# Layer norms of finished rows moved from VectorE to ScalarE and GpSimd in the second-last expert list, and their stores to GpSimd's queue

## The chip, the cores and the metric

The kernel runs on one core of a Trainium2 chip. The metric is device time in microseconds, the median of three runs. The core's engines each work through a queue of their own in order and wait for each other by semaphores: TensorE (PE, with its weight loads as PEld), VectorE (DVE), ScalarE (ACT), GpSimd (POOL), and SyncE (SP), which here only begins transfers.

## The reference

Two layers of an encoder, 512 tokens of width 1024 in float32. What matters here is the end of the second layer, a mixture of experts:

```
x = layer_norm(DN_ALPHA * x + mix, ln_attn_g[i], ln_attn_b[i])
ffn = moe_swiglu(x, w_router[j], b_router[j], w_exp_in[j], w_exp_out[j])   # top 2 of 8 experts
x = layer_norm(DN_ALPHA * x + ffn, ln_ffn_g[i], ln_ffn_b[i])

def layer_norm(x, g, b):
    mu  = mean(x);  var = mean((x - mu) ** 2)
    return (x - mu) * rsqrt(var + LN_EPS) * g + b
```

Each token goes to two of the eight experts; an expert is a SwiGLU with weights of 1024 x 5632 and 2816 x 1024 in float32.

## The kernel before

**Lists.** Tokens are gathered by expert into eight lists of at most CAP[s] rows (160, 128, 152, 134, 144, 140, 168, 128), and the kernel works list by list. List 6 (L6 = LAST - 1) has 168 places, in two blocks of 128 and 40 rows, and list 7 (LAST) has 128.

**Weights.** All weights are streamed from HBM in chunks of 1 MB (128 x 2048 float32, tile raw). SP begins a load when a raw buffer is free. ACT rounds a chunk to float16 (wh, L149), DVE makes the remainder (wl, L158: raw x 256 minus wh), each in two pieces of 1048 and 1000 columns, and PE does three float16 products for each float32 one. DVE's wl also frees the raw buffer. In list 6 and 7 a list has 22 chunks for the gate and up product (block4 and quad: lines 1442 to 1444) and 11 or 12 for the down product (down_wide, lines 1471 to 1473; down_direct, lines 1517 to 1519, in list 7).

**Activations of a list.** For four columns blocks at a time ACT takes Silu out of PSUM (sa, L1457), DVE multiplies by the up half (L1458), ACT rounds to float16 (act, L231), and GpSimd makes the remainder (L1460). sa has two buffers, so ACT's L1457 waits for a L1460 of two quads earlier.

**Ends of lists.** A list's rows are scaled and added to a table in HBM, expert_sums, by an indirect DMA from GpSimd (add_rows, L1375). When list 6 begins, expert_sums holds lists 0 to 5. In list 6 GpSimd adds it to all four token tiles (token_sums), DVE takes their statistics (stats), and norm_out(t) norms each tile of 128 tokens and stores it to the output. That is done at four places in list 6's program: with its last gate pair and with its first three groups of the down product. The tokens of list 6 and list 7 get wrong values there and are written again: rows_done(L6, i) norms the rows of list 6 after their own down product and writes them over the output (L1691, indirect), at two places in list 7's down product, and rows_done(LAST, 0) does so for list 7 at the very end.

**The two ways to norm.** `inverse` makes 1/sqrt(var + eps): a Sqrt on ACT and five tiny operations on DVE. Then, in halves of 512 columns:

```
def centred(o, mean, inv, gb, n):          # on DVE: (o - mean) * g, then (o * inv) + b
    for h in range(2):
        centre(o, mean, gb, n, h)          # L442
        stretch(o, inv, gb, n, h)          # L446
def shared(o, mean, inv, gb, n=128):       # off = -mean * inv on DVE (L456), then for each half
    nc.scalar.activation(o[:, c], o[:, c], AF.Identity, bias=off, scale=inv)    # L459, ACT
    nc.gpsimd.tensor_mul(o[:, c], o[:, c], gb[0][:n, c])                        # L460, GpSimd
    nc.gpsimd.tensor_add(o[:, c], o[:, c], gb[1][:n, c])                        # L461, GpSimd
```

`shared` is used before already, for two token tiles of the first layer and through norm_rows(..., spread=True). The order of every engine's work is that of the program: nothing reorders it.

Of the kernel before, what the change touches and what calls it, by code (L numbers as in the profile page):

```python
# [56 lines left out]
LAST = NEXP - 1  # L57
# [152 lines left out]
def trunk_kernel(ctx, tc, x, mem, positions, w_in_swa, attn_sinks, w_in_fox, b_forget, w_mem_kv, w_out,  # L210
                 ln_attn_g, ln_attn_b, w_ffn_in, w_ffn_out, w_router, b_router, w_exp_in, w_exp_out,
                 ln_ffn_g, ln_ffn_b, out):
    nc = tc.nc
# [117 lines left out]
    xtok = base.tile([128, NT, D], FT, name="xtok")  # L331
# [76 lines left out]
    def ln_load(lnp, g, b, eng=nc.scalar, **kw):  # L408
        t = []
        for name, w in (("lng", g), ("lnb", b)):  # L410
            o = lnp.tile([128, D], FT, **(kw or {"name": name}))
            eng.dma_start(o, bass.AP(tensor=w.tensor, offset=w.offset, ap=[[0, 128], [1, D]]))
            t.append(o)
        return t
# [11 lines left out]
    def inverse(w, var, s, between=()):  # L426

        between = list(between)
        nc.scalar.activation(w[:, 1], var, AF.Sqrt, bias=eps[s][:var.shape[0]])
        nc.vector.tensor_scalar(w[:, 0], var, EPS / (s * s), None, op0=OP.add)  # L430
        for f in between[:1]:
            f()
        nc.vector.reciprocal(w[:, 1], w[:, 1])
        for f in between[1:]:
            f()
        nc.vector.tensor_mul(w[:, 2], w[:, 1], w[:, 1])
        nc.vector.scalar_tensor_tensor(w[:, 2], w[:, 2], -0.5, w[:, 0], op0=OP.mult, op1=OP.mult)
        nc.vector.scalar_tensor_tensor(w[:, 3], w[:, 2], 1.5, w[:, 1], op0=OP.add, op1=OP.mult)

    def centre(o, mean, gb, n, h):  # L440
        c = slice(h * 512, h * 512 + 512)
        nc.vector.scalar_tensor_tensor(o[:, c], o[:, c], mean, gb[0][:n, c], op0=OP.subtract, op1=OP.mult)  # L442

    def stretch(o, inv, gb, n, h):
        c = slice(h * 512, h * 512 + 512)
        nc.vector.scalar_tensor_tensor(o[:, c], o[:, c], inv, gb[1][:n, c], op0=OP.mult, op1=OP.add)  # L446

    def centred(o, mean, inv, gb, n):
# [4 lines that stand above are left out]
    def shared(o, mean, inv, gb, n=128):  # L453

        off = small.tile([128, 1], FT, name="off")[:n]
        nc.vector.scalar_tensor_tensor(off, mean, -1.0, inv, op0=OP.mult, op1=OP.mult)  # L456
        for h in range(2):
            c = slice(h * 512, h * 512 + 512)
            nc.scalar.activation(o[:, c], o[:, c], AF.Identity, bias=off, scale=inv)  # L459
            nc.gpsimd.tensor_mul(o[:, c], o[:, c], gb[0][:n, c])  # L460
            nc.gpsimd.tensor_add(o[:, c], o[:, c], gb[1][:n, c])  # L461

    def norm_rows(o, st, s, gb, n, spread=False):
        mv = small.tile([128, 2], FT, name="mv")[:n]
        nc.vector.bn_aggr(mv, st)
        w = small.tile([128, 4, 1], FT, name="lnw")[:n]
        if spread:
            inverse(w, mv[:, 1:2], s)
            shared(o, mv[:, 0:1], w[:, 3], gb, n)
        else:  # L470
            inverse(w, mv[:, 1:2], s, [lambda h=h: centre(o, mv[:, 0:1], gb, n, h) for h in range(2)])
            for h in range(2):
                stretch(o, w[:, 3], gb, n, h)
# [507 lines left out]
    gb = ln_load(fp, ln_ffn_g[0], ln_ffn_b[0])  # L981
# [3 lines left out]
    for r in range(0, S + CMAX, 128):  # L985
        m = min(128, S + CMAX - r)
# [338 lines left out]
    def small_t(name, shape, dt=FT):  # L1325
        return me.tile(shape, dt, name=name)
# [5 lines left out]
    def blocks(s):  # L1332
        return [(r, min(128, CAP[s] - r)) for r in range(0, CAP[s], 128)]
# [307 lines left out]
    gbx = ln_load(mx, ln_ffn_g[1], ln_ffn_b[1])  # L1641
# [15 lines left out]
    X = {}  # L1657
# [29 lines left out]
    def rows_done(s, i, st, to):  # L1687

        m = blocks(s)[i][1]
        norm_rows(X[s][i][:m, :], st[:m, :], 1.0, gbx, m)  # L1690
        nc.gpsimd.indirect_dma_start(out=out[0], out_offset=bass.IndirectOffsetOnAxis(ap=to[:m, i:i + 1], axis=0),  # L1691
                                     in_=X[s][i][:m, :], in_offset=None, bounds_check=S - 1, oob_is_err=False)

# [3 lines left out]
    mvs = small_t("mvs", [128, NT, 2])  # L1697
    lnw = small_t("lnw4", [128, 4, NT])
# [5 lines left out]
        nc.vector.bn_aggr(mvs[:, t, :], st)  # L1704

    def norm_out(t, gb):
        centred(xtok[:, t, :], mvs[:, t, 0:1], lnw[:, 3, t:t + 1], gb, 128)
        nc.scalar.dma_start(out[0, t * 128:(t + 1) * 128, :], xtok[:, t, :])

    jobs = {}  # L1710

# [6 lines left out]
    for t in range(NT):  # L1718
        at(L6, 5, lambda t=t: token_sums(t))
        at(L6, 7 if t < 2 else 8, lambda t=t: stats(t))  # L1720
        at(L6, 10 + t, lambda t=t: norm_out(t, gbx))
    at(L6, 9, lambda: inverse(lnw, mvs[:, :, 1], 1.0))
    at(L6, 9, lambda: residual(LAST, rows))
    for i in range(len(blocks(L6))):
        at(LAST, 11 + i, lambda i=i: rows_done(L6, i, st6[:, i, :], at_[L6][1]))
# [7 lines left out]
    for s in range(NEXP):  # L1733
# [41 lines left out]
        else:  # L1775
            for gi, u in enumerate(u_eo[s]):
# [17 lines left out]
                for f in jobs.get((s, 11 + gi), ()):  # L1794
                    f()
    late_work()
    rows_done(LAST, 0, st7, at_[LAST][1])
    mxx.close()

# [4 lines left out]
    with tc.If(nit > 0, preferred_fallthrough_block=False):  # L1804
# [77 lines left out]
        gbx = ln_load(lp, ln_ffn_g[1], ln_ffn_b[1])  # L1882
# [6 lines left out]
        for t in range(NT):  # L1889
            norm_out(t, gbx)  # L1890
# [26 lines left out]
```

## Time and profile before

| | |
|---|---|
| median of 3 runs | 1634.07 us (1633.24 to 1634.15) |
| the profiled execution: its time, its span | 1634.23 us, 1632.4 us |
| PE busy | 1578.6 us (97%) |
| DVE busy | 1210.9 us (74%) |
| ACT busy | 950.3 us (58%) |
| POOL busy | 267.7 us (16%) |

All times of rows are microseconds from the start of the span. The shares are means over stages with different limits: DVE's 74% is near 100% in the last lists. The chain that the page follows back from the last instruction is cut off after the last store, so the end is read from the stages instead. PE's busy time counts overlapping matmuls; a gap in it is real.

### The profile page before, as it was taken

The numbers are of one execution on the slowest core, as the hardware profiler recorded it, in microseconds if no ns is written. First come the engines' busy times: TensorE is split into PE (matmuls) and PEld (weight loads), VectorE is DVE, ScalarE is ACT, GpSimd is POOL, SyncE is SP. The second block draws the span as 40 slices with busy tenths as digits, with TensorE's granted clock in tenths as the row PEclk, the third lists the DMA queues.
The fourth block names the chain that finished last, engine by engine and source line by source line (L and its number), as shares of the span: only waits on it lengthen the run. The fifth ranks groups of instructions, "written<-read, shape, count | busy, mean of one in ns | idle before, by whom it ended". The sixth has DMA issues, their size and how long they took to land. (4 is left out here: it accounts for less than half of the span.)

```text
span 1632.4 us, 42978 instructions
## 1 busy us (share of the span) xinstructions
PE 1578.6 (97%) x18640; PEld 1267.8 (78%) x18640; DVE 1210.9 (74%) x1811; ACT 950.3 (58%) x1447; POOL 267.7 (16%) x264
## 2 busy tenths in 40 slices
PE   7998999999999999999899999999999999999996
PEld 6775654444444747765899999999999999999984
DVE  6798543333634568787898798888979889699997
ACT  6676243333211356663676787767877678666773
POOL 0443100000200000003120330203112030130251
PEclk9999999999999999999999999999999999999998
DMA  7511043332631132201899899999999999999993
GB/s 275 178 53 53 27 129 104 103 104 91 219 114 60 53 129 92 66 27 65 308 363 364 293 394 377 352 370 305 390 357 361 375 320 373 329 297 360 358 369 113
DMA packets 180549, 370.16 MB, mean 227 GB/s; under 512 B 6589, under 2 KB 49597, under 8 KB 180352
## 3 DMA queue, kind: packets, MB, share of 16 engines
q1 hardware_dynamic: 173280, 343.48, 58.6%
q0 software_dynamic: 4768, 15.47, 4.0%
q10 hardware_dynamic: 2304, 8.39, 1.4%
q8 instruction: 148, 2.42, 0.6%
q14 instruction: 49, 0.40, 0.1%
HBM read 355.08 MB, written 12.39 MB: 225 GB/s over the span
## 5 line engine op out<-in xcount | busy, mean ns | idle before, releaser
L158 DVE SCALAR_TENSOR_TENSOR wl<-raw,wh 128x1048 f16<-128x1048 f32 (+3 forms) x658 | 794.7, 1258 | 100.3 <-ACT wh L149 100.1
L149 ACT ACTIVATE wh<-raw 128x1048 f16<-128x1048 f32 (+3 forms) x658 | 641.8, 1036 | 101.7 <-PE bk L239 42.9
L1444 PE MATMUL bk<-xa,wl 128*128 128x160 f16 (+3 forms) x1280 | 260.0, 231 | 0.9 <-DVE wl L158 0.9
L1442 PE MATMUL bk<-xa,wh 128*128 128x160 f16 (+3 forms) x1280 | 260.1, 231 | 0.8 <-ACT xa L231 0.8
L1443 PE MATMUL bk<-xa,wh 128*128 128x160 f16 (+3 forms) x1280 | 260.0, 231 | 0.0
L1443 PEld LDWEIGHTS <-wh 128*128 128x128 f16 x2560 | 250.5, 98 | 3.6 <-issue 2.4
L1444 PEld LDWEIGHTS <-wl 128*128 128x128 f16 x2560 | 250.5, 98 | 1.3 <-DVE wl L158 1.1
L1442 PEld LDWEIGHTS <-wh 128*128 128x128 f16 x2560 | 250.4, 98 | 0.7
L1473 PE MATMUL bk<-act,wl 128*128 128x160 f16 (+6 forms) x1232 | 235.3, 227 | 1.2 <-DVE wl L158 1.2
L1472 PE MATMUL bk<-act,wh 128*128 128x160 f16 (+6 forms) x1232 | 235.3, 227 | 0.0
L1471 PE MATMUL bk<-act,wh 128*128 128x160 f16 (+6 forms) x1232 | 235.2, 227 | 0.0
L1442 PE MATMUL bk<-xe,wh 128*128 128x128 f16 (+2 forms) x1280 | 223.2, 221 | 2.2 <-DVE sa L1458 1.4
L1443 PE MATMUL bk<-xe,wh 128*128 128x128 f16 (+2 forms) x1280 | 223.1, 221 | 0.0
L1444 PE MATMUL bk<-xe,wl 128*128 128x128 f16 (+2 forms) x1280 | 223.1, 221 | 0.0
L237 PE MATMUL bk<-xTh,wh 128*128 128x512 f16 (+2 forms) x656 | 204.8, 322 | 1.2 <-DVE Kx L234 0.9
L239 PE MATMUL bk<-xTh,wl 128*128 128x512 f16 (+2 forms) x656 | 204.6, 322 | 1.4 <-DVE wl L158 1.4
L238 PE MATMUL bk<-xTl,wh 128*128 128x512 f16 (+2 forms) x656 | 204.6, 322 | 0.5 <-DVE xTl L234 0.5
L1460 POOL TENSOR_TENSOR act<-sa,act 128x512 f16<-128x512 f32 (+6 forms) x40 | 106.3, 2659 | 284.7 <-ACT act L231 284.6
L239 PEld LDWEIGHTS <-wl 128*128 128x128 f16 x944 | 92.4, 98 | 49.0 <-DVE wl L158 2.9
L237 PEld LDWEIGHTS <-wh 128*128 128x128 f16 x944 | 92.4, 98 | 48.7 <-ACT wh L149 2.0
L238 PEld LDWEIGHTS <-wh 128*128 128x128 f16 x944 | 92.5, 98 | 46.6 <-issue 1.5
L1473 PEld LDWEIGHTS <-wl 128*128 128x128 f16 x1232 | 120.5, 98 | 1.6 <-DVE wl L158 1.6
(349 smaller groups left out, 2669.2 us busy)
## 6 DMA issues: line engine op xcount, KB each, us to landing
raw<-in_w_exp_in_dram SPq DMA_DIRECT2D x176, 1024.0 KB
raw<-in_w_exp_out_dram SPq DMA_DIRECT2D x85, 1024.0 KB
raw<-in_w_ffn_in_dram SPq DMA_DIRECT2D x22, 1024.0 KB
raw<-in_w_out_dram SPq DMA_DIRECT2D x8, 1024.0 KB
raw<-in_w_ffn_out_dram SPq DMA_DIRECT2D x8, 1024.0 KB
raw<-in_w_in_fox_dram SPq DMA_DIRECT2D x8, 1024.0 KB
raw<-in_w_in_swa_dram SPq DMA_DIRECT2D x4, 896.0 KB
raw<-in_w_mem_kv_dram SPq DMA_DIRECT2D x3, 1024.0 KB
```

The lines of the kernel that those rows point to most:

```text
L149: self.nc.scalar.activation(h[:, p:e], t[:, p:e], AF.Copy, scale=SW)
L158: self.nc.vector.scalar_tensor_tensor(l, src, SW, h, op0=OP.mult, op1=OP.subtract)
L237: nc.tensor.matmul(o, lh, rh, start=first, stop=False, **kw)
L238: nc.tensor.matmul(o, lh, rl, start=False, stop=False, **kw)
L239: nc.tensor.matmul(o, ll, rh, start=False, stop=last, **kw)
L1442: nc.tensor.matmul(o, wh[:, k, c], xe[0][:, k, :C], start=first, stop=False, skip_group_check=True)
L1443: nc.tensor.matmul(o, wh[:, k, c], xe[1][:, k, :C], start=False, stop=False, skip_group_check=True)
L1444: nc.tensor.matmul(o, wl[:, k, c], xe[0][:, k, :C], start=False, stop=k == KD - 1, skip_group_check=True)
L1460: lambda: nc.gpsimd.tensor_sub(act[1][:, j, :C], sa[:, :, :C], act[0][:, j, :C])]
L1471: nc.tensor.matmul(o, wh[:, k, c], act[0][:, kk, :C], start=first, stop=False, skip_group_check=True)
L1472: nc.tensor.matmul(o, wh[:, k, c], act[1][:, kk, :C], start=False, stop=False, skip_group_check=True)
L1473: nc.tensor.matmul(o, wl[:, k, c], act[0][:, kk, :C], start=False, stop=kk == KF - 1, skip_group_check=True)
```

## The change

Two edits. The norm of the four token tiles uses `shared` in place of `centred`, and the store of each tile is begun by GpSimd in place of ACT. And rows_done uses `shared` (spread) for list 6's rows, but not for list 7's.

```diff
     def rows_done(s, i, st, to):
         m = blocks(s)[i][1]
-        norm_rows(X[s][i][:m, :], st[:m, :], 1.0, gbx, m)
+        norm_rows(X[s][i][:m, :], st[:m, :], 1.0, gbx, m, s < LAST)
         nc.gpsimd.indirect_dma_start(out=out[0], ...
...
     def norm_out(t, gb):
-        centred(xtok[:, t, :], mvs[:, t, 0:1], lnw[:, 3, t:t + 1], gb, 128)
-        nc.scalar.dma_start(out[0, t * 128:(t + 1) * 128, :], xtok[:, t, :])
+        shared(xtok[:, t, :], mvs[:, t, 0:1], lnw[:, 3, t:t + 1], gb)
+        nc.gpsimd.dma_start(out[0, t * 128:(t + 1) * 128, :], xtok[:, t, :])
```

DVE at the first token tile, in list 6's last gate pair (xtok is the token tile, mvs and lnw its mean and inverse, lng and lnb the norm's weights):

```order
 L158 SCALAR_TENSOR_TENSOR wl<-raw,wh 128x1000
 L158 SCALAR_TENSOR_TENSOR wl<-raw,wh 128x1048
-L442 SCALAR_TENSOR_TENSOR xtok<-xtok,mvs,lng 128x512
-L446 SCALAR_TENSOR_TENSOR xtok<-xtok,lnw_8950,lnb 128x512
-L442 SCALAR_TENSOR_TENSOR xtok<-xtok,mvs,lng 128x512
-L446 SCALAR_TENSOR_TENSOR xtok<-xtok,lnw_8950,lnb 128x512
+L456 SCALAR_TENSOR_TENSOR off<-mvs,lnw_8950 128x1
 L158 SCALAR_TENSOR_TENSOR wl<-raw,wh 128x1000
```

One tiny operation stands where four of 128 x 512 stood; the same holds at the other three tiles, each of which has four wl between it and the next.

GpSimd from list 6's last remainders of act to list 6's rows (the four tiles' pieces are alike; the last tile's end is shown):

```order
+L460 TENSOR_TENSOR xtok<-xtok,lng 128x512
+L461 TENSOR_TENSOR xtok<-xtok,lnb 128x512
+L460 TENSOR_TENSOR xtok<-xtok,lng 128x512
+L461 TENSOR_TENSOR xtok<-xtok,lnb 128x512
+L1708 DMA out_dram<-xtok 128x1024
+L1375 DMA expert_sums<-yr,to 680x1024 x2
+L1460 TENSOR_TENSOR act_23021<-sa,act_23020 128x4x128 x2
 L1683 DMA xg_21598<-expert_sums,idx 128x1024
```

Sixteen operations and four stores now stand in GpSimd's queue ahead of list 6's additions to expert_sums, list 7's remainders of act and list 7's fetch of its sums.

DVE at the second block of list 6's rows, in list 7's down product (xg holds the block's 40 rows):

```order
 L465 BN_AGGR mv<-st_8947 40x2
 L430 TENSOR_SCALAR lnw<-mv 40x1
-L442 SCALAR_TENSOR_TENSOR xg_19598<-xg_19598,mv,lng 40x512
 L433 RECIPROCAL lnw<-lnw 40x1
-L442 SCALAR_TENSOR_TENSOR xg_19598<-xg_19598,mv,lng 40x512
 L436 TENSOR_TENSOR lnw<-lnw 40x1
 L437 SCALAR_TENSOR_TENSOR lnw<-lnw 40x1
 L438 SCALAR_TENSOR_TENSOR lnw<-lnw 40x1
-L446 SCALAR_TENSOR_TENSOR xg_19598<-xg_19598,lnw,lnb 40x512 x2
+L456 SCALAR_TENSOR_TENSOR off<-mv,lnw 40x1
 L158 SCALAR_TENSOR_TENSOR wl<-raw,wh 128x1048
```

The big four leave DVE here too, and with them what DVE did while the Sqrt ran on ACT; on ACT two L459 now stand between that Sqrt and the next wh.

## Rows read from the trace of the kernel before

**Rows 1.** Windows: list 6's down product, list 7's gate, list 7's down product.

```profile
core 0: us, PE busy (x) PEld busy (x) DVE busy (x) ACT busy (x) POOL busy (x), PEclk, DMA share, GB/s
1482.30:1522.10 39.80, 38.56 (x530) 38.16 (x528) 36.49 (x40) 21.85 (x24) 0.00 (x0) 1.00 0.94 338
1522.10:1585.30 63.20, 61.05 (x1075) 60.71 (x1073) 60.42 (x59) 51.19 (x63) 32.93 (x8) 1.00 1.05 366
1585.30:1620.70 35.40, 30.96 (x202) 19.89 (x198) 31.69 (x50) 19.51 (x27) 7.37 (x3) 0.95 0.50 186
```

**Rows 2.** Waits, 1482 to 1621: who waited for whom, total us, times, longest.

```profile
PE bk L1518 <- DVE wl L158: 4.4, 3, 3.9
...
ACT sa L1457 <- POOL act L1460: 3.2, 1, 3.2
...
PE bk L1473 <- DVE wl L158: 1.2, 2, 0.9
```

**Rows 3.** Timeline of PE in list 7's down product: longest wait, last matmul.

```profile
1605.66 0.27 PE L1518 MATMUL bk<-wl,act 128*128 128x256 f16 x1 [3.89 <-DVE wl L158]
...
1620.39 0.27 PE L1519 MATMUL bk<-wh,act 128*128 128x256 f16 x1
```

**Rows 4.** Timeline of DVE, list 7's last quads and list 6's finished rows.

```profile
1574.15 9.16 DVE L158 SCALAR_TENSOR_TENSOR wl<-raw,wh 128x1000 f16<-128x1000 f32 x8
1583.23 0.68 DVE L1458 SCALAR_TENSOR_TENSOR sa<-bk,sa 128x512 f32<-128x512 f32 x1
...
1594.38 0.20 DVE L465 BATCH_NORM_AGGREGATE mv<-st 128x2 f32<-128x12 f32 x1
...
1597.97 2.93 DVE L158 SCALAR_TENSOR_TENSOR wl<-raw,wh 128x488 f16<-128x488 f32 x3
1600.82 0.19 DVE L465 BATCH_NORM_AGGREGATE mv<-st 40x2 f32<-40x12 f32 x1
...
1604.38 4.61 DVE L158 SCALAR_TENSOR_TENSOR wl<-raw,wh 128x1048 f16<-128x1048 f32 x4
...
1612.35 4.08 DVE L158 SCALAR_TENSOR_TENSOR wl<-raw,wh 128x1048 f16<-128x1048 f32 x4
```

**Rows 5.** DVE's timeline at the second token tile (start, us, instructions, idle before).

```profile
1495.34 0.75 DVE L442 SCALAR_TENSOR_TENSOR xtok<-xtok,mvs,lng 128x512 f32<-128x512 f32 x1
...
1498.24 1.20 DVE L158 SCALAR_TENSOR_TENSOR wl<-raw,wh 128x1000 f16<-128x1000 f32 x1
1499.92 3.52 DVE L158 SCALAR_TENSOR_TENSOR wl<-raw,wh 128x1048 f16<-128x1048 f32 x3 [0.48 <-ACT wh L149]
```

**Rows 6.** Source L149, 1490 to 1526 (ns min/median/max; first and last start).

```profile
L149 ACT ACTIVATE wh<-raw x23: 1019/1060/1077, 1490.4 to 1525.0; 128x1048 f16<-128x1048 f32 x12, 128x1000 f16<-128x1000 f32 x11
```

**Rows 7.** Timeline of a shared norm in the first layer: ACT, then POOL.

```profile
149.10 0.29 ACT L429 ACTIVATE lnw<-mv,eps 128x1 f32<-128x1 f32 x1 [2.39 <-DVE mv L465]
150.41 1.52 ACT L459 ACTIVATE xtok<-xtok,off,lnw 128x512 f32<-128x512 f32 x2 [1.01 <-DVE off L456]
...
151.30 1.27 POOL L460 TENSOR_TENSOR xtok<-xtok,lng 128x512 f32<-128x512 f32 x1 [4.85 <-ACT xtok L459]
```

**Rows 8.** Timeline of POOL, list 6's last remainder and list 7.

```profile
1480.44 1.55 POOL L1460 TENSOR_TENSOR act<-sa,act 128x672 f16<-128x672 f32 x1 [15.16 <-ACT act L231]
1530.04 2.47 POOL L1375 DMA_INDIRECT expert_sums<-yr,to  x1 [48.05 <-ACT yr L1493]
1541.47 10.41 POOL L1375 DMA_INDIRECT expert_sums<-yr,to  x1 [8.95 <-issue]
...
1574.97 9.36 POOL L1460 TENSOR_TENSOR act<-sa,act 128x512 f16<-128x512 f32 x1 [9.26 <-ACT act L231]
```

**Rows 9.** Sources L158 (at 1480.6 and 1583.8) and L1460 (whole span), columns as before.

```profile
L158 DVE SCALAR_TENSOR_TENSOR wl<-raw,wh x1: 2517/2517/2517, 1480.6 to 1480.6; 128x1048 f16<-128x1048 f32 x1
...
L158 DVE SCALAR_TENSOR_TENSOR wl<-raw,wh x1: 1554/1554/1554, 1583.8 to 1583.8; 128x1000 f16<-128x1000 f32 x1
...
L1460 POOL TENSOR_TENSOR act<-sa,act x40: 1150/1518/9356, 812.9 to 1584.7; 128x512 f16<-128x512 f32 x10, 128x640 f16<-128x640 f32 x5, 128x608 f16<-128x608 f32 x5, 128x536 f16<-128x536 f32 x5
```

## The prediction, on record before the run

> **What bounds the kernel now.** I read the windows of the last three stages first [rows 1]. In list 6's down product PE is busy 38.56 of 39.80 us, in list 7's gate 61.05 of 63.20, in its down product 30.96 of 35.40. DVE stands close beside it: 36.49, 60.42 and 31.69. The DMA share is near 1 in the first two. So no engine has much to spare. PE idles 1.24 + 2.15 + 4.44 = 7.8 us in all, and that is the most that relief for DVE can give back from PE's side (plus a little clock: the granted share falls to 0.95 in the last window).
>
> The waits say what ends PE's idle time: wl, twice in list 6's down product and three times in list 7's, the longest 3.9 us [rows 2]. PE's timeline puts that one at 1605.66 [rows 3]. DVE's own timeline shows what made wl late [rows 4]: list 6's finished rows took DVE from 1594.38 to 1597.97 and from 1600.82 to 1604.38, and the wl for which PE waits stands behind them. From there on PE follows DVE: the last wl ends at 1612.35 + 4.08 = 1616.4, PE's last matmul starts at 1620.39. How much of these 4.0 us must come after the wl the rows don't show; I give PE 1 us in hand there (bounds 0 and 2). What comes behind 1620.7 is list 7's own norm, which the change leaves alone. So the account is DVE's: what it gains or loses between 1482 and 1616 arrives at the end, less that 1 us.
>
> The sum is made against the profiled execution, 1634.23, which stands 0.16 above the median of the runs. A measurement of this kernel can hardly tell less than 0.2%, some 3.3 us, from no change.
>
> **Edit 1, the four token tiles.**
>
> *Removed from DVE.* One tile's norm lies between 1495.34 and 1498.24, 2.9 us [rows 5]. Four of them: -11.6.
>
> *Added to DVE.* Four off of 128 x 1. A tiny operation takes 0.2 [rows 4]: +0.8.
>
> *Added to ACT.* The pair of L459 took 1.52 [rows 7], in place of the store's issue. ACT itself has time (21.85 busy of 39.80 [rows 1]). But the pair waits for DVE's off, and the next wh are queued behind it, and DVE's next wl but one waits for a wh. After off DVE has one wl of 1.20 in hand [rows 5], while ACT needs 1.52 for the pair and 1.06 for a wh [rows 6]: DVE idles 1.52 + 1.06 - 1.20 = 1.4. Today it idles 0.48 at that place [rows 5], because the store on ACT waits for the norm. So +0.9 a tile, +3.6 (bounds 0, if ACT is already a wh ahead, and +5.6, if all of the 1.4 is new).
>
> *Added to GpSimd.* Sixteen operations of 1.27 [rows 7] and four stores. They run where POOL is busy for 0.00 of 39.80 us [rows 1], so their own length costs nothing. Their price is what they do to DVE's wl. At 1480.44 a remainder of 1.55 us ran on GpSimd [rows 8] and the wl beside it took 2.517 in place of about 1.2: 1.3 more, 0.84 of GpSimd's time [rows 9]. For an operation of 1.27 that is 1.07. GpSimd can lose, too: the remainder at 1574.97 lasted 9.36 us [rows 8] over eight wl in a row and came to its end only when DVE turned to L1458 [rows 4]; the wl behind that one took 1.554, only 0.35 more [rows 9]. The median of the 40 remainders is 1.518 against a longest of 9.356 [rows 9], so most get in quickly and I count two of three at 1.07 and one at 0.35: 0.85 for each operation that meets a wl. DVE runs wl nearly without a break here, so I let 12 of 16 meet one: +10.2 (bounds 0 and 16 x 1.07 = +17).
>
> On this the Trainium skill has a rule ("SBUF — State Buffer", section "Who interferes with whom"): a DVE instruction with two SBUF inputs contends with a GpSimd instruction that reads SBUF, the lock is exclusive, and whichever was issued first holds it for its whole length while the other blocks fully. The trace agrees that one blocks the other (2.517 beside 1.55), but not that order of issue alone decides, since the one at 1574.97 was passed over by wl issued after it. By the rule each of the 12 would cost the full 1.07, 12.8 in place of 10.2.
>
> *The stores.* GpSimd's queue is in order, and each tile's store waits for that tile's last L461; the next tile's operations are queued behind it. The bytes are the same and POOL is otherwise empty until L1375 at 1530.04 [rows 8], so I cost them at nothing; without that cover they belong to the third rival.
>
> Sum of edit 1 on DVE: -11.6 + 0.8 + 3.6 + 10.2 = +3.0.
>
> **Edit 2, list 6's own rows.** The two stretches are 3.59 and 3.56 [rows 4]. Not all of it goes: the aggregate (0.20), the Sqrt on ACT (0.29) and the tiny operations up to off (1.01 [rows 7]) stay, about 1.5, with nothing left on DVE to fill them. Freed: 2 x 2.1 = -4.2. Two L459 on ACT again precede the next wh, with the same gap of 1.4 and no idle time at that place now: +2.8 (bounds 0 and 2.8). Eight operations on GpSimd, of which I let 6 meet a wl: 6 x 0.85 = +5.1 (bounds 0 and 8.6). The write to the output (L1691) comes a few microseconds later, and nothing waits for it before list 7's rows are through. Sum: +3.7.
>
> **Total.** DVE +6.7, less 1 in hand: +5.7, 1634.2 + 5.7 = **about 1640**. The sum changes its sign with the number n of the 24 operations that meet a wl. Without them it is -11.6 + 0.8 + 3.6 - 4.2 + 2.8 = -8.6; 8.6 / 0.85 = 10, with PE's 1 us in hand 11. I count 18. Own range: 14 to 22 of 24, or +2.3 to +9.1: 1636.5 to 1643.5.
>
> **Rivals.**
>
> *1. Faster.* The operations fall into DVE's gaps, the new ones behind off above all, or run beside its L1458 and its adds, and fewer than 7 meet a wl. Then DVE saves some 3 to 8 us and PE's waits of 7.8 shrink [rows 1]. PE's longest gap of 3.89 [rows 3] goes, with its slow matmuls (its granted clock of 0.95 says that a part of that window ran at 1.2 in place of 2.4 GHz [rows 1]): 1634 - 7 = about 1627. For it: the removed 11.6 + 4.2 are certain, the added price isn't. Against: DVE is busy 36.49 of 39.80 and 31.69 of 35.40, so there are few gaps.
>
> *2. No change.* 8 to 12 meet, or ACT is a wh ahead at the tiles (the +3.6 falls away) while the locks cost what I say: 1634 ± 3.
>
> *3. GpSimd starves and becomes the bound.* What happened at 1574.97 happens to half of the sixteen, at some 5 us each (between 1.27 and 9.36 [rows 7, 8]), and the others wait for half a wl: 16 x (0.5 x 5 + 0.5 x 1.9) = 55 us. The first tile comes four wl and a norm, 4 x 1.2 + 2.9 = 7.7, before the second one's 1495.3 [rows 5], so at 1488, and GpSimd is done at 1543. L1375 wants POOL at 1530.04 and list 7's remainders are behind it; ACT's L1457, which already waits 3.2 for them [rows 2], and PE behind it would be some 12 later: about 1646. A start of L1375 also took 10.41 in place of 2.47 among wl [rows 8], so the four stores could add to it. Against: the median of 1.518, and that off and the gap behind it open the lock at every tile.
>
> *4. Strict turns.* Each operation gets in behind the wl that runs, none starves, and each of 18 costs 1.07: 19.3 in place of 15.3, total +9.7, about 1644. The row of 9.36 speaks against it. It is what the rule of the Trainium skill above ("SBUF — State Buffer", "Who interferes with whom") would make of the time.
>
> **Numbers.** My forecast 0.42, strict turns 0.08, starving 0.14, no change 0.18, faster 0.18. The point is the likeliest case's, 1640. The range 1630 to 1647 leaves out most of the faster cases (0.13) and the worst of the starving ones (0.07). Slower by over 0.2%: 0.42 + 0.08 + 0.14 = 0.64, with a little of it within 0.2% and as much of the no-change case beyond it.
>
> **What would show it.** In the new trace: wl of about 2.2 to 2.5 us wherever a L460 or L461 runs beside one, some 12 of them in list 6's down product; DVE idle for 1.4 behind each off, released by ACT's wh; PE's waits for wl in list 6's down product above 1.2 in total; no wait of 3.9 at L1518 but several shorter ones; POOL done with the four tiles before 1530. I am wrong if most wl keep 1.2 (rival 1), if L1375 starts late (rival 3), or if PE never waits for the delayed wl, because it is further behind DVE in list 6 than I take it to be: then edit 1 costs nothing and only edit 2's +3.7 is left.

## The result and the profile after

The change makes the kernel slower: median 1643.3 us (1642.65 to 1646.25, 4 runs) against 1633.65 (1633.15 to 1634.15, 4 runs), ratio 1.006 with a 95% interval of 1.0047 to 1.0072. That is +9.7 us, where the prediction said +5.7 and a range of 1630 to 1647.

The windows of the changed kernel, at the same places of the program as [rows 1], with the end as a fourth:

```profile
core 0 of [0], span 1644.5 us
core 0: us, PE busy (x) PEld busy (x) DVE busy (x) ACT busy (x) POOL busy (x), PEclk, DMA share, GB/s
1484.10:1527.20 43.10, 39.07 (x530) 38.05 (x528) 36.07 (x27) 30.66 (x36) 30.51 (x21) 1.00 0.83 296
1527.20:1592.60 65.40, 62.41 (x1076) 62.09 (x1074) 65.26 (x63) 51.90 (x64) 32.01 (x8) 0.97 1.05 369
1592.60:1629.40 36.80, 31.95 (x201) 20.45 (x198) 30.40 (x41) 21.18 (x29) 19.72 (x11) 0.91 0.46 172
1629.40:1644.50 15.10, 0.00 (x0) 0.00 (x0) 4.51 (x12) 0.77 (x2) 1.00 (x1) 0.63 0.08 31
```

All four stages are longer: 43.1 for 39.8, 65.4 for 63.2, 36.8 for 35.4, and the end, of which the prediction said that the change leaves it alone, 15.1 for 11.7. DVE's busy time in the first window hardly fell (36.07 for 36.49) although four norms of 2.9, 11.6 us in all, left it.

DVE's timeline from the second tile to the third (as [rows 5]), and POOL's beside it:

```profile
1498.60 0.15 DVE L456 SCALAR_TENSOR_TENSOR off<-mvs,lnw 128x1 f32<-128x1 f32 x1
1498.67 1.19 DVE L158 SCALAR_TENSOR_TENSOR wl<-raw,wh 128x1000 f16<-128x1000 f32 x1
1501.31 6.58 DVE L158 SCALAR_TENSOR_TENSOR wl<-raw,wh 128x1048 f16<-128x1048 f32 x3 [1.45 <-ACT wh L149]
1507.81 0.15 DVE L456 SCALAR_TENSOR_TENSOR off<-mvs,lnw 128x1 f32<-128x1 f32 x1
```

```profile
1499.69 1.30 POOL L460 TENSOR_TENSOR xtok<-xtok,lng 128x512 f32<-128x512 f32 x1 [2.75 <-ACT xtok L459]
1501.07 1.27 POOL L461 TENSOR_TENSOR xtok<-xtok,lnb 128x512 f32<-128x512 f32 x1
1502.30 2.29 POOL L460 TENSOR_TENSOR xtok<-xtok,lng 128x512 f32<-128x512 f32 x1
1504.67 2.11 POOL L461 TENSOR_TENSOR xtok<-xtok,lnb 128x512 f32<-128x512 f32 x1
1507.08 0.59 POOL L1708 DMA_DIRECT2D out_dram<-xtok  x1 [0.30 <-POOL xtok L461]
```

One wl follows off, then DVE idles 1.45 until ACT has done its two L459 and a wh (forecast: 1.4). GpSimd's first operation falls into that gap. The other three meet the three wl that follow: these take 6.58 in place of 3.52 [rows 5], 1.02 more for each operation, and GpSimd's own grow from 1.27 to 2.1 and 2.3. Both engines lose when they overlap. None of the 16 tile operations took more than 2.3, so none waited for more than one wl. (GpSimd's spans are rough in the profile; DVE's are the firmer ones.)

The rows of list 6 on DVE, in list 7's down product (as [rows 4]), to the last four wl:

```profile
1599.50 0.19 DVE L465 BATCH_NORM_AGGREGATE mv<-st 128x2 f32<-128x12 f32 x1
...
1600.84 0.16 DVE L456 SCALAR_TENSOR_TENSOR off<-mv,lnw 128x1 f32<-128x1 f32 x1
1600.91 0.66 DVE L158 SCALAR_TENSOR_TENSOR wl<-raw,wh 128x488 f16<-128x488 f32 x1
1603.55 4.29 DVE L158 SCALAR_TENSOR_TENSOR wl<-raw,wh 128x1048 f16<-128x1048 f32 x2 [1.97 <-ACT wh L149]
...
1612.12 6.60 DVE L158 SCALAR_TENSOR_TENSOR wl<-raw,wh 128x1000 f16<-128x1000 f32 x3 [1.33 <-ACT wh L149]
...
1622.08 4.08 DVE L158 SCALAR_TENSOR_TENSOR wl<-raw,wh 128x1048 f16<-128x1048 f32 x4
```

From the aggregate to the wl behind off it is 1.4 (forecast: 1.5), the gaps are 1.97 and 1.33, and the five wl behind them take 10.89 (4.29 + 6.60) where five of 1.2 would take 6.0.

PE's waits from 1480 to 1632 (as [rows 2]):

```profile
PE bk L1518 <- DVE wl L158: 4.1, 2, 2.1
PE bk L1473 <- DVE wl L158: 3.8, 3, 1.8
PE bk L1442 <- DVE sa L1458: 3.0, 1, 3.0
```

The wait of 3.89 [rows 3] is gone, two of 2.1 and 2.0 stand in its place, the waits of list 6's down product have grown from 1.2 [rows 2] to 3.8, and PE's wait for DVE's sa, at the start of list 7's gate, from 1.4 to 3.0. ACT's wait of 3.2 for GpSimd's remainder [rows 2] no longer occurs.

Last, the end. Source L1804 is the branch behind list 7's norm; with this input no list overflows and the block behind it is skipped. EVENT_SEMAPHORE is a wait, and INC_SWDGE_SEM sets the semaphores of GpSimd's transfers forward. GpSimd's rows there, in the changed kernel (ns min/median/max, first and last start):

```profile
L1804 POOLq EVENT_SEMAPHORE  x5: 17/43/2525, 1634.8 to 1635.2; - x5
...
L1804 POOLq INC_SWDGE_SEM  x1: 1187/1187/1187, 1637.7 to 1637.7; - x1
```

In the kernel before:

```profile
L1804 POOLq EVENT_SEMAPHORE  x4: 17/43/43, 1626.1 to 1626.4; - x4
...
L1804 POOLq INC_SWDGE_SEM  x1: 1122/1122/1122, 1626.5 to 1626.5; - x1
```

Before, there were four such waits of at most 43 ns, and the INC_SWDGE_SEM followed 0.8 after the start of list 7's write (L1691, 1625.7). Now a fifth wait of 2.5 us stands between; it ends at 1637.7, and that write landed 3.2 us after its start at 1634.4.

**One account of the two traces.** Three marks on DVE and GpSimd cut the stretch: DVE's first tile, its last four wl, the start of list 7's L1691. From the first tile to the last four wl before took 1612.35 - 1485.30 = 127.05; now 1622.08 - 1488.83 = 133.25: +6.2. From there to list 7's L1691: 1634.41 - 1622.08 = 12.3, before 13.35: -1.0. From there to the end of the span: 10.1, before 6.7: +3.4. Together +8.6. The profiled execution is 3.5 later already at the first tile (1488.83 for 1485.30), ahead of every changed instruction: ACT's L1457 stood 1.8 later at 1441.47 (before: 1439.68), and after that ACT waited 6.8 for raw data at 1466.8 (before: 2.3). This 3.5 is not the change's: e2 below, with the same instructions up to there, reaches the first tile at 1485.88. 3.5 + 8.6 = 12.1 is the difference of the spans, 1644.5 - 1632.4. The medians differ by 9.7; single runs spread over some 3 us.

### The profile page after: what moved, and what is told of

Same layout as the page of the kernel before. It is cut to its first block, busy times and chain, and to the rows that moved or that the text cites. A ratio compares the mean times of both kernels' runs of the same rounds, so it can differ in the third digit from the quotient of the medians.

```text
span 1644.5 us, 43009 instructions
## 1 busy us (share of the span) xinstructions
PE 1582.9 (96%) x18640; PEld 1270.4 (77%) x18640; DVE 1211.9 (74%) x1793; ACT 959.5 (58%) x1459; POOL 307.5 (19%) x292
## 5 line engine op out<-in xcount | busy, mean ns | idle before, releaser
L158 DVE SCALAR_TENSOR_TENSOR wl<-raw,wh 128x1048 f16<-128x1048 f32 (+3 forms) x658 | 810.9, 1282 | 107.1 <-ACT wh L149 107.0
L149 ACT ACTIVATE wh<-raw 128x1048 f16<-128x1048 f32 (+3 forms) x658 | 642.1, 1036 | 97.2 <-PE bk L239 42.4
L1473 PE MATMUL bk<-act,wl 128*128 128x160 f16 (+6 forms) x1232 | 235.4, 227 | 4.0 <-DVE wl L158 3.8
L1460 POOL TENSOR_TENSOR act<-sa,act 128x512 f16<-128x512 f32 (+6 forms) x40 | 114.2, 2854 | 290.5 <-ACT act L231 290.3
L1473 PEld LDWEIGHTS <-wl 128*128 128x128 f16 x1232 | 120.5, 98 | 5.1 <-DVE wl L158 5.1
```

What stands on the lines that cost most here:

```text
L149: self.nc.scalar.activation(h[:, p:e], t[:, p:e], AF.Copy, scale=SW)
L158: self.nc.vector.scalar_tensor_tensor(l, src, SW, h, op0=OP.mult, op1=OP.subtract)
L1460: lambda: nc.gpsimd.tensor_sub(act[1][:, j, :C], sa[:, :, :C], act[0][:, j, :C])]
L1473: nc.tensor.matmul(o, wl[:, k, c], act[0][:, kk, :C], start=False, stop=kk == KF - 1, skip_group_check=True)
```

## Experiments

Theory: DVE's wl are held up where GpSimd's multiplications and additions read the same memory, by about 1 us each, and by the gap behind off; PE follows DVE at the end; and the end itself is longer because of the stores. Rivals: ScalarE's extra work is what costs; PE's slack hides the tiles; the longer end is chance. The table gives, for each run, the account above: M from DVE's first tile to its last four wl (in e8 without the block that is moved behind them), N from there to list 7's L1691, T from there to the end of the span, each against before (127.05, 13.35, 6.7), their sum, and the time as a ratio to the kernel before on the same chip (1634.5 and 1634.4 there).

| run | M | N | T | sum | ratio (95%) |
|---|---|---|---|---|---|
| changed kernel | +6.2 | -1.0 | +3.4 | +8.6 | 1.0060 (1.0047 to 1.0072) |
| e1, skipped block's stores | 0.0 | -0.2 | +3.2 | +3.0 | 1.0018 (1.0009 to 1.0027) |
| e2, changed, block on ACT | +6.2 | -1.4 | +0.9 | +5.7 | 1.0033 (1.0022 to 1.0043) |
| e3, tiles only | +1.6 | -1.4 | +0.8 | +1.0 | 1.0012 (1.0003 to 1.0021) |
| e4, rows only | +4.6 | -1.4 | +0.6 | +3.8 | 1.0018 (1.0009 to 1.0027) |
| e5, no GpSimd work | -3.5 | +0.3 | +0.4 | -2.8 | 0.9973 (0.9961 to 0.9985) |
| e6, memset | -3.5 | +0.3 | +0.8 | -2.4 | 0.9974 (0.9963 to 0.9985) |
| e7, lock alone | +10.9 | -0.6 | +0.4 | +10.7 | 1.0069 (1.0055 to 1.0082) |
| e8, rows behind last wl | -3.5 | 0.0 | 0.0 | -3.5 | 0.9982 (0.9973 to 0.9991) |

T varies by up to 0.9 between runs whose ends are alike; only e1 and the changed kernel stand apart from that. The trace of e3 is that of its fastest run (1633.86, against a median of 1636.91).

### e1: the stores in the block that is skipped

```diff
-    def norm_out(t, gb):
+    def norm_out(t, gb, queue=nc.scalar):
...
-        nc.scalar.dma_start(out[0, t * 128:(t + 1) * 128, :], xtok[:, t, :])
+        queue.dma_start(out[0, t * 128:(t + 1) * 128, :], xtok[:, t, :])
...
         for t in range(NT):
-            norm_out(t, gbx)
+            norm_out(t, gbx, nc.gpsimd)
```

> The kernel before, but the four stores in the block behind the branch at the program's end, which this input skips, are begun by GpSimd; everything that runs is as before. Theory (skipped block): GpSimd then has to wait for list 7's last write before it closes the skipped block, and the tail from that write's start to the end grows from 6.7 to about 10.1 us: +2.5 to +3.4, about 1636.5. Rival (the longer tail comes from the stores that run, or is chance): no change, 1633.7, tail 6.7.

1638.5 us, ratio 1.0018: DVE's work is where it was (M 0.0) and the kernel is slower by 2.9 us by the ratio, by 4.0 by the medians (expected: 2.5 to 3.4). The skipped block calls norm_out too. GpSimd's program at the branch, before (-) and in this run (+), with the semaphores that each row waits for (ISA is the INC_SWDGE_SEM, together with the waits ahead of it):

```
 L1804 COMPARE_AND_BRANCH
-L1804 ISA [waits Pool_49,DMASW4_49,DMASW3_49,DMASW6_49,DMASW2_49,DMASW7_49,DMASW1_49,DMASW0_49]
+L1804 ISA [waits Pool_49,DMASW4_49,DMASW5_49,DMASW3_49,DMASW6_49,DMASW2_49,DMASW7_49,DMASW1_49,DMASW0_49]
```

GpSimd's transfers take eight semaphores in turn (DMASW0 to 7). On the way round the block GpSimd sets forward those that the block would have used, and first waits for each of them. Before, the block had seven such transfers, which left out one semaphore, DMASW5, and that was the one of list 7's last write. With four stores more the block uses all eight. The source view of L1804 in this run:

```profile
L1804 POOLq EVENT_SEMAPHORE  x5: 17/43/43, 1625.8 to 1629.2; - x5
...
L1804 POOLq INC_SWDGE_SEM  x1: 1107/1107/1107, 1629.3 to 1629.3; - x1
```

The waits stretch from 1625.8 to 1629.2, and the INC_SWDGE_SEM comes 3.9 after the start of list 7's write (1625.4, landed 3.7 later) in place of 0.8; what follows moves with it.

### e2: the changed kernel with that block's stores left to ScalarE

```diff
-    def norm_out(t, gb):
+    def norm_out(t, gb, queue=nc.gpsimd):
...
-        nc.gpsimd.dma_start(out[0, t * 128:(t + 1) * 128, :], xtok[:, t, :])
+        queue.dma_start(out[0, t * 128:(t + 1) * 128, :], xtok[:, t, :])
...
         for t in range(NT):
-            norm_out(t, gbx)
+            norm_out(t, gbx, nc.scalar)
```

> The changed kernel, with the skipped block's four stores left to ScalarE. Theory (skipped block): the tail falls back from 10.1 to 6.7 us and nothing else moves: 1643.3 - 3 = about 1640. Rival: 1643. Either way 11 to 13 of the 16 tile operations on GpSimd meet a wl and the stretch of DVE from list 6's last gate pair to the end of its down product is about 3.3 us longer than before.

1640.4, ratio 1.0033. The long wait is gone again, M is the changed kernel's to 0.1:

```profile
L1804 POOLq EVENT_SEMAPHORE  x4: 17/43/43, 1631.5 to 1631.7; - x4
...
L1804 POOLq INC_SWDGE_SEM  x1: 1197/1197/1197, 1631.8 to 1631.8; - x1
```

So the long wait belongs to the stores that don't run. With those that run T is +0.9, which is within what T varies by. In list 6's down product 11 wl took over 1.6 us (before: none), as expected.

### e3 and e4: one edit at a time

e3 is e2 with rows_done of before:

```diff
-        norm_rows(X[s][i][:m, :], st[:m, :], 1.0, gbx, m, s < LAST)
+        norm_rows(X[s][i][:m, :], st[:m, :], 1.0, gbx, m)
```

> Edit 1 alone (the tiles by ScalarE and GpSimd, their stores by GpSimd; the skipped block's stores by ScalarE so that the tail stays short); list 6's rows by DVE as before. Theory (wl late by the lock, no slack on PE): DVE +3.3 us over the four tiles, PE later by about as much: 1636 to 1637. Rival (PE's slack of 2 to 4 us in list 7's gate takes it up): within 1 us of 1633.7.

e4 is the kernel before with the other edit alone:

```diff
-        norm_rows(X[s][i][:m, :], st[:m, :], 1.0, gbx, m)
+        norm_rows(X[s][i][:m, :], st[:m, :], 1.0, gbx, m, s < LAST)
```

> Edit 2 alone (list 6's rows by ScalarE and GpSimd), tiles by DVE as before. Theory: two gaps of about 1.5 us behind off and six or seven wl longer by about 1 us: DVE +4 to +4.6, time 1637 to 1638.5. Rival (the two stretches of 3.6 us that go from DVE are what PE waits for, so PE gains): 1630.

e3: 1636.9, 1.0012, so +2.0 by the ratio: between the two expectations and nearer to the first. e4: 1637.7, 1.0018, as the theory said. Their ratios add up to 1.0030, e2 has 1.0033. PE's waits in e3, then in e4:

```profile
PE bk L1473 <- DVE wl L158: 2.5, 2, 1.8
PE bk L1518 <- DVE wl L158: 2.4, 2, 2.1
```

```profile
PE bk L1518 <- DVE wl L158: 5.7, 4, 1.8
...
PE bk L1473 <- DVE wl L158: 1.3, 2, 0.9
```

The tiles make PE wait earlier (2.5 at L1473 for 1.2) and less later (2.4 at L1518 for 4.4 [rows 2]): part of PE's delay in list 6 is swallowed by the wait that comes anyway in list 7. What is left of it is what DVE is late by there, and DVE gets half of the tiles' price back (below).

### e5 and e6: GpSimd's operations left out, or made to read nothing

In e5 the two lines of GpSimd are left out in `shared` for the four tiles and list 6's rows (the output lacks g and b there); in e6 memset of the same columns stands for each (the output there is zero).

```diff
-    def shared(o, mean, inv, gb, n=128):
+    def shared(o, mean, inv, gb, n=128, bare=False):
...
             nc.scalar.activation(o[:, c], o[:, c], AF.Identity, bias=off, scale=inv)
-            nc.gpsimd.tensor_mul(o[:, c], o[:, c], gb[0][:n, c])
-            nc.gpsimd.tensor_add(o[:, c], o[:, c], gb[1][:n, c])
+            if not bare:
+                nc.gpsimd.tensor_mul(o[:, c], o[:, c], gb[0][:n, c])
+                nc.gpsimd.tensor_add(o[:, c], o[:, c], gb[1][:n, c])
+            for _ in range(2 * bare):
+                nc.gpsimd.memset(o[:, c], 0.0)
```

(The last two lines are e6's only. The four tiles and list 6's rows pass bare=True.)

> As e2_block_on_act, but GpSimd's multiplication by g and addition of b are left out for the four tiles and list 6's rows (so the output lacks g and b there); ScalarE's part, the gaps behind off and all stores stay. Theory (the lock is what costs): the wl keep 1.2 us, DVE loses 11.6 + 4.2 us and gains 0.8 + 4 to 5 of gaps at the tiles and 2.8 at the rows, net -8; PE's waits for wl shrink: 1628 to 1631. Rival (what costs is ScalarE, whose two L459 delay the next wh): as e2, 1639 to 1641.

> As e5_no_gpsimd_work, but in place of each left out multiplication and addition GpSimd sets the same 512 columns to zero, an operation that writes and reads nothing (the output of these rows is zero before later rows are written over it). Theory (GpSimd's reads and DVE's second input exclude each other): no wl above 1.3 beside these, time as e5, 1628 to 1631. Rival (any GpSimd operation on the same memory holds DVE up): wl of 2 us and more, time as e2, about 1640.

1630.5 and 1631.0, ratios 0.9973 and 0.9974: both faster than before, by the same, though ScalarE does all that it does in e2 and the gaps of 1.45 behind off are there. The wl of e6 in list 6's down product (source L158 from 1484 to 1528), and the four memsets of a tile on POOL:

```profile
L158 DVE SCALAR_TENSOR_TENSOR wl<-raw,wh x27: 1183/1195/1252, 1483.2 to 1527.3; 128x1000 f16<-128x1000 f32 x14, 128x1048 f16<-128x1048 f32 x13
```

```profile
1494.84 2.15 POOL L464 MEMSET xtok<- 128x512 f32 x4 [5.28 <-ACT xtok L459]
```

No wl is longer than 1.252. So ScalarE is not the cost; GpSimd's multiplications and additions are. That they cost because they read is shown by few events: a memset takes 0.52 where a multiplication takes 1.27, and 14 of the 24 memsets (16 at the tiles, 8 at the rows) lie wholly where DVE runs no wl, most of them in the gap behind off. Five lie beside a wl for nearly their whole length, at 1496.46, 1502.61, 1508.75, 1595.89 and 1602.16, and five more for 0.2 to 0.3. None of these wl took longer than 1.252, where a wait would have added up to 0.5. The time of e6 says no more than that of e5. DVE came out 3.5 earlier at its last wl, not 8 as the theory counted: with the wl at their old length DVE runs out of work (in e6 it idles 4.2 ahead of list 6's first join) and being earlier brings no more.

### e7: the lock alone

```diff
     def norm_out(t, gb):
         centred(xtok[:, t, :], mvs[:, t, 0:1], lnw[:, 3, t:t + 1], gb, 128)
+        for h in range(2):
+            for _ in range(2):
+                nc.gpsimd.tensor_mul(spill, xtok[:, t, h * 512:h * 512 + 512], gb[0][:, h * 512:h * 512 + 512])
         nc.scalar.dma_start(out[0, t * 128:(t + 1) * 128, :], xtok[:, t, :])
...
+    spill = small_t("spill", [128, 512], FH)
```

> The kernel before, and behind each of the four tile norms GpSimd multiplies four times 512 columns of the tile by g into a scratch tile that nobody reads (half-precision result): 16 GpSimd operations without any work taken from DVE or given to ScalarE. Theory (lock): nearly all 16 meet a wl and make it about 1.0 us longer, DVE +13 to +16 in list 6's down product; with some 1.5 us that PE has in hand at the end and up to 2 that DVE gets back in list 7's gate: 1643 to 1647. Rival (GpSimd's work lies beside DVE's): 1634.

1645.5, ratio 1.0069: 16 operations that nobody waits for cost 11 us. POOL at the second tile, the wl from 1484 to 1528, and PE's wait:

```profile
1498.46 7.74 POOL L1710 TENSOR_TENSOR spill<-xtok,lng 128x512 f16<-128x512 f32 x4 [4.22 <-issue]
```

```profile
L158 DVE SCALAR_TENSOR_TENSOR wl<-raw,wh x15: 1234/2259/2317, 1483.6 to 1525.9; 128x1048 f16<-128x1048 f32 x8, 128x1000 f16<-128x1000 f32 x7
```

```profile
PE bk L1473 <- DVE wl L158: 10.5, 4, 3.5
```

The median wl is 2.26 for 1.2, and PE's waits in list 6's down product are 10.5 for 1.2. DVE's stretch from the first tile to list 6's first join is 12.6 longer (expected: 13 to 16), and 1.7 of it comes back in list 7's gate (expected: up to 2).

### e8: list 6's second block behind the last wl

```diff
     L6 = LAST - 1
+    LATE = (0, 3)
...
-        at(LAST, 11 + i, lambda i=i: rows_done(L6, i, st6[:, i, :], at_[L6][1]))
+        at(LAST, 11 + LATE[i], lambda i=i: rows_done(L6, i, st6[:, i, :], at_[L6][1]))
```

> The kernel before, with the norm of list 6's second block of rows moved from the second to the fourth place of list 7's down product, which puts it behind DVE's last wl. Theory (DVE's 3.56 us between two wl is what PE's 3.9 us wait in list 7's down product is made of, and DVE idles 3.3 us behind its last wl): the wait falls below 1.5 and the time to 1631 to 1632.5. Rival (the 3.56 us then delay DVE's last joins by as much): no change or up to 2 slower.

1631.4, ratio 0.9982 (0.9973 to 0.9991): faster than both kernels, as expected. DVE's end and PE's wait:

```profile
1607.99 4.08 DVE L158 SCALAR_TENSOR_TENSOR wl<-raw,wh 128x1048 f16<-128x1048 f32 x4
1611.99 0.19 DVE L465 BATCH_NORM_AGGREGATE mv<-st 40x2 f32<-40x12 f32 x1
...
1615.55 0.47 DVE L1506 SCALAR_TENSOR_TENSOR xg<-bk,g,xg 128x256 f32<-128x256 f32 x1
```

```profile
PE bk L1518 <- DVE wl L158: 0.9, 3, 0.3
```

The 3.56 us of the second block now fill the time in which DVE idled behind its last wl, and PE's longest wait in that stage is 0.3 for 3.9. With the wait the fall of PE's clock is gone: the granted clock of the same stage is 1.00 here, against 0.95 before [rows 1], where it fell to 1.2 GHz right behind the wait of 3.89.

## Why the prediction held, and what it missed

**Direction and mechanism: right, and shown.** Without GpSimd's multiplications and additions (e5, and e6 with memsets) e2 would be faster than the kernel before; with them it is slower; and such operations alone (e7) cost 11 us. The Trainium skill ("SBUF — State Buffer", section "Who interferes with whom") draws the line where these runs find it: two SBUF inputs on DVE against a GpSimd instruction that reads, not one that only writes. e6 agrees, with 1.252 as the longest wl, in the ten memsets that touch one. No run varied DVE's side, but the changed kernel's trace agrees there too: DVE's L1409, one of whose inputs is in PSUM, took 0.51 at 1492.33 with an addition and then a multiplication beside it, as without them (0.51 at 1490.52 in the kernel before).

**DVE's sum: +6.7 forecast, +6.2 measured,** but by other parts, so that it came so near is partly luck. The first tile to list 6's first join took 46.5 for 43.2, +3.3 (forecast for edit 1: +3.0; 11 operations of 16 met a wl for 12 and cost 10.6 for 10.2, and the gaps are 1.45 for 1.4). From there to the aggregate of list 6's rows DVE was 1.7 quicker than before, which the forecast didn't have: in the kernel before, ACT waited 3.2 for a remainder of GpSimd [rows 2] and DVE 2.7 for the wh behind it; with DVE later at list 6's join this wait is absent in the changed kernel. It goes with the delay and not with the norms: e7, which moves no norm and is 12.6 late there, lacks the wait and gains the same 1.7, as do e2 and e3 (3.3 late), while e1, e4, e5, e6 and e8, none of them late there, all keep the 3.2. From the aggregate to the last four wl it took 22.6 for 18.0, +4.6 (forecast for edit 2: +3.7; the gaps are 1.97 + 1.33 = 3.3 for 2.8, and all five wl that met one cost about a full microsecond more).

**PE's time in hand:** 1 forecast, 1.0 in the changed kernel, 1.4 in e2 to e4. With it the prediction's terms give 6.2 - 1.4 = +4.8 and, with 0.9 of T, e2's +5.7; e2's ratio, 1.0033, is +5.4. The forecast of +5.7 is met by e2, not by the changed kernel; the range was wide enough for both.

**The step that was mis-sized** is "The stores ... I cost them at nothing", and with it "list 7's own norm, which the change leaves alone". The queue past which I moved the stores was looked at, and there they did cost nothing: L1375 started at 1534.64 and had waited 8.59 for ACT's yr, not for POOL. But the same function is called a second time, in the block that is skipped, and four more GpSimd transfers there make GpSimd wait for list 7's write before it can end: 2.5 of the +3.4 of T in the trace, and +3.2 in e1. The other 0.9 of T stands in e2 without that wait, so it is not the block's; its cause is open. Of the 4.0 by which the medians exceed the forecast (9.7 - 5.7) the wait is 2.5 to 3.2, and the rest is within the spread of single runs.

**The rivals.** Starving (3) did not happen: every tile operation got in behind the wl that ran, and POOL was done with the tiles at 1526 against 1530 forecast as the limit. Strict turns (4) describes the tiles and the rows better than my "two of three": each operation that met a wl cost about 1. Only 16 met one in place of 18, so they came to about what I had counted, and that rival's +9.7, about 1644, is reached by luck: it has nothing of the skipped block. Nor does it describe list 7's remainders in the same trace, three of which were passed over, for 9.41, 9.36 and 5.40 us, until DVE turned to an operation with an input in PSUM (L1458 or L1409):

```profile
1549.02 9.41 POOL L1460 TENSOR_TENSOR act<-sa,act 128x512 f16<-128x512 f32 x1
...
1569.78 9.36 POOL L1460 TENSOR_TENSOR act<-sa,act 128x512 f16<-128x512 f32 x1 [6.69 <-ACT act L231]
...
1590.47 5.40 POOL L1460 TENSOR_TENSOR act<-sa,act 128x512 f16<-128x512 f32 x1 [9.26 <-ACT act L231]
```

The Trainium skill's rule that order of issue decides (same page and section) therefore fits the new operations, 16 of which met a wl, and not these three; what makes the difference is open.

## What to carry to other kernels

Work that is moved from a busy VectorE to an idle GpSimd is not free where VectorE streams operations with two SBUF inputs: price each GpSimd operation that meets one at most of its own length on VectorE (here 1.02 for 1.27), add the gap that the handover leaves, and compare that with what was removed (here 2 to 3 times 1.0 and a gap 1.0 longer, against 2.9 a tile). Before work is moved to another engine, look for a place on the same engine behind its last critical operation (e8). And where a function is edited, look up all its calls: a branch that is never taken still has bookkeeping, and its semaphores can put a wait on the way round it.

## What the runs showed of the hardware

- The way round a skipped block took 2.5 (changed kernel) and 3.2 us longer (e1) where the block's GpSimd transfers, eleven of them, used all eight semaphores, the last write's among them; with seven transfers, which left that one out (before, e2), it did not.
- GpSimd and DVE slow each other: beside wl an operation of 1.27 took 2.1 to 2.3 on GpSimd while each wl went from 1.2 to between 2.1 and 2.3. In e7 DVE's L446 beside GpSimd went from 0.75 to 1.64, too.
- PE's granted clock in the last stage was 0.95 with one wait of 3.9 (before), 0.91 with two of 2.1 and 2.0 (changed kernel) and 1.00 with three of at most 0.3 (e8). The waits alone don't tell it: in e3 it was 1.00 with two, of 2.1 and 0.3 (1585.3 to 1620).
